# Attention with 10 of 17 blocks turned by TensorE, second key copies made by GpSimd, values in three 64-column products, and feed-forward weights at another remainder mod 512

## The chip, the cores and the metric

The kernel runs on one core of a Trainium2 chip. The metric is device microseconds of one execution, the median of the runs shown. Engine names are those of the profile: PE (TensorE matmul), PEld (TensorE weight load), DVE (VectorE), ACT (ScalarE), POOL (GpSimd), SP (SyncE, which issues most of the DMAs). Line numbers with an L are those of the kernel before.

## The reference, cut to what matters

One decoder layer for 2048 tokens of width 1024: a projection, eight attention heads of width 64 with a forget bias, a short gated convolution, an output projection, and a convolutional feed-forward of width 2816.

```python
logits = einsum('bqhd,bkhd->bhqk', qb, kb) * scale            # 128 queries, keys up to them
logits = logits + fcum[:, :, q0:q1, None] - fcum[:, :, None, :q1]
p = softmax(where(causal, logits, -inf))                      # over the key prefix
out = einsum('bhqk,bkhd->bqhd', p, vb)
...
u = causal_dwconv(h2 @ w_up, ffn_conv_w); y = (silu(u_gate) * u_val) @ w_down
```

Everything is float32. The kernel gets that precision by splitting an operand into a high and a low part (float32r for keys, queries and weights, float16 for the softmax weights and the values) and adding three products: high by high, high by low, low by high.

## The kernel before

**Stages.** The projections and the short convolution run to about 623 us of the span, attention from there to about 1025 us, the output projection (`mixed`, L853) with the second norm to about 1265 us, then twice the feed-forward's first product (`up`, L972, line L983 on PE) and second product (`down`, L1065, line L140 on PE).

**Attention's units.** A head is cut into 8 units. Unit `u` holds query block 15-u and query block u, which together have 17 blocks of 128 keys, so all 64 units have the same amount of work: five score chunks of up to 512 keys, 17 weight blocks of 128 x 128.

**Attention's steps.** The loop of L773 runs a software pipeline: in step `s` the generator `turn` works on unit s-2, `scores` on unit s, `weights` on unit s-1, `values` on unit s-4, a piece each in turn. `K` (L136) keeps the instructions of each engine in this program order; DMAs on SP are not pinned.
- `scores` (L672): `product` (L655) makes for each chunk two float32r products, L664 (key high parts) and L665 (key low parts), and a mask L667 for the last chunk. The contraction has 128 rows: rows 0 to 63 meet the query's high part, rows 64 to 127 its low part, so `kh` and `kl` hold the same 64 rows twice. Four PSUM banks (`ps_s`). DVE adds the forget bias `nf` and takes the running maximum (L688).
- `weights` (L698): ACT makes the exponential in place (L705).
- `turn` (L711): the 17 blocks of a unit must be transposed, in float16 high and low parts. The first `WB` = 6 go by PE (L726) into a PSUM bank of `ps_x` (two banks), ACT rounds the high part into `near` (L728), DVE makes the low part from the PSUM bank and the high part (L733), which frees the bank. The other 11 go another way: ACT (L709, the first 128 columns) and POOL (L718) round the high parts into `wide`, POOL subtracts for the low parts (L719), and one transposing DMA on SP (L720) carries both into `far`.
- `values` (L737): for each block a 128-column product of the high weights with the values' high and low parts side by side (L747) and a 64-column product of the low weights with the values' high part (L748). ACT scales the result into `at` (L752); its two 64-column halves are added later by DVE in `store` (L759), then transposed by PE (L764) and written out.

**Loads of the next head.** `load_head` (L557) gives seven DMAs on SP: `kh` twice, `qs` high and low, `kl` twice (64 x 2048 each, 512 KB) and `nf` (one row spread over 128 partitions, 1 MB). L787 issues one at each step u = 1 to 7 of the head before. The tiles have two buffers.

**Placement.** SBUF tiles on the right side lie below an `edge` tile of 32 bytes (L73). In the built program the feed-forward's weight tiles `hi` and `lo` (L825) start at remainder 448 mod 512 bytes, the operands `b11` to `t4` of `up` at remainder 0. In `down` and `mixed` both operands are halves of `hi` and `lo` tiles.

Of the kernel before, what the change touches and what calls it, by code (L numbers as in the profile page):

```python
# [19 lines left out]
P = 128  # L20
# [14 lines left out]
WB = 6  # L35
XA = 128
# [8 lines left out]
def kernel(  # L45
# [27 lines left out]
    edge.tile([P, 8], F32, name="edge")  # L73
# [73 lines left out]
    with ExitStack() as ph:  # L147
# [221 lines left out]
        p_ = bp.tile(n, F32, name="p_", bufs=1)  # L369
# [12 lines left out]
        V.scalar_tensor_tensor(p_, p_, -2.0, e_, op0=ALU.mult, op1=ALU.add)  # L382
        tri = bp.tile(n, F32, name="tri", bufs=1)
# [15 lines left out]
        def running_sum():  # L399
            pc = ps_t.tile([P, 512], F32, tag="tr", name="pc")  # L400
            K(T.matmul(pc[:, 0:P], lhsT=p_, rhs=tri, start=True, stop=True))
            V.tensor_copy(cum, pc[:, 0:P])
# [154 lines left out]
        def load_head(h):  # L557

            pr, r0 = h // 2, (h % 2) * DH
            r1 = r0 + DH  # L560
            tiles, loads = [], []
            for tag, srcs in (("kh", (k_hi, k_hi)), ("qs", (q_hi, q_lo)), ("kl", (k_lo, k_lo))):
                t = sp.tile([P, S], F32R, tag=tag, name=tag)
                for n, src in enumerate(srcs):
                    loads.append((t.bitcast(F32)[n * DH : (n + 1) * DH, :], src[r0:r1, pr, :]))
                tiles.append(t)
            t = sp.tile([P, S], F32, tag="nf", name="nf")
            loads.append((t, nf_sc[h].partition_broadcast(P)))
            return (*tiles, t), loads

        def issue(load):
            nc.sync.dma_start(*load)


        for j in range(4):
# [10 lines left out]
            for ch in range(4):  # L586
                if j == 3 and ch == 2:
                    hap.__exit__(None, None, None)
                    sp = st.enter_context(tc.tile_pool(name="sp", bufs=2, side="right"))
                    head, loads = load_head(0)  # L590
                    for ld in loads:
                        issue(ld)
# [34 lines left out]
    with ExitStack() as ph:  # L627
# [70 lines left out]
        def weights(un):  # L698

            s_t = un["s"]  # L700
            nb = cs.tile([P, 2], F32, tag="nb", name="nb")
            K(A.activation(nb, un["mx"], AF.Copy, scale=-1.0, bias=LN_PS))
            for p, (_, n, b0) in enumerate(un["parts"]):
                cols = s_t[:, b0 * P : (b0 + n) * P]
                K(A.activation(cols, cols, AF.Exp, bias=nb[:, p : p + 1], accum_out=un["l"][:, p : p + 1]))  # L705
                yield
            un["wide"] = wide = cp.tile([P, 2, WU - WB * P], F16, tag="wide", name="wide", bufs=3)
            if XA:
                K(A.activation(wide[:, 0, 0:XA], s_t[:, WB * P : WB * P + XA], AF.Copy))  # L709

        def turn(un):  # L711
# [6 lines left out]
            K(G.tensor_scalar(wide[:, 0, XA:], s_t[:, WB * P + XA : WU], 1.0, 0.0, op0=ALU.mult, op1=ALU.add))  # L718
# [3 lines left out]
            for b0 in range(0, WB, 4):  # L722
                nb = min(4, WB - b0)
                pt = ps_x.tile([P, 512], F32, tag="x", name="pt")
                for b in range(nb):
                    K(T.transpose(pt[:, b * P : (b + 1) * P], s_t[:, (b0 + b) * P : (b0 + b + 1) * P], ident))  # L726
                th, tl = [near[:, a, b0 : b0 + nb, :].rearrange("p b n -> p (b n)") for a in range(2)]
                K(A.activation(th, pt[:, 0 : nb * P], AF.Copy))  # L728
                late.append((tl, pt[:, 0 : nb * P], th))
            yield  # L730
            yield
            for tl, pt, th in late:
                K(V.tensor_tensor(tl, pt, th, op=ALU.subtract))  # L733
                yield
            K(V.reciprocal(un["l"], un["l"]))

        def values(un):  # L737
# [3 lines left out]
            for p, (i, n, b0) in enumerate(un["parts"]):  # L741
                po = ps_o.tile([P, P], F32, tag="o", name="po")
                for b in range(n):
# [3 lines left out]
                    K(T.matmul(po, lhsT=t[:, 0, :], rhs=v, start=b == 0, stop=False))  # L747
                    K(T.matmul(po[:, 0:DH], lhsT=t[:, 1, :], rhs=v[:, 0:DH], start=False, stop=b == n - 1))  # L748
                    if b % 4 == 3:
                        yield  # L750
                o = un["at"][:, i, :, (h % 2) * DH : (h % 2 + 1) * DH]
                K(A.activation(o, po.rearrange("p (a d) -> p a d", a=2), AF.Copy, scale=un["l"][:, p : p + 1]))  # L752
                yield

        def store(at, pr, chs):

            parts = [at[:, ch * 4 : ch * 4 + 4, :, :] for ch in chs]
            for part in parts:
                K(V.tensor_tensor(part[:, :, 0, :], part[:, :, 0, :], part[:, :, 1, :], op=ALU.add))  # L759
                yield  # L760
            for ch, part in zip(chs, parts):
                pt = ps_x.tile([P, 512], F32, tag="x", name="pt")
                for t in range(4):
                    K(T.transpose(pt[:, t * P : (t + 1) * P], part[:, t, 0, :], ident))  # L764
# [8 lines left out]
        for s in range(H * nu + 8):  # L773
            h, u = divmod(s, nu)
            run = []
            if h < H:
                if u == 0:
                    loads = []
                    if h + 1 < H:
                        heads[h + 1], loads = load_head(h + 1)  # L780
                    if h % 2 == 0:
                        if h:
                            v16.append(load_values(h // 2))
                        at = cp.tile([P, NT, 2, P], F32, tag="at", name="at")
# [342 lines left out]
```

## Time and profile before

| | |
|---|---|
| runs shown | 2614.63, 2619.37, 2624.09 us (median 2619.37) |
| the profiled execution, its own time | 2621.2 us |
| its span in the profile | 2619.5 us, so 1.7 us lie around it |
| PE busy | 2463.2 us, 94% of the span |
| DVE, ACT, POOL busy | 1800.2, 1142.5, 360.4 us |
| mean DMA rate | 161 GB/s |

Busy time of PE is a count of pipelined instructions, so 94% is not 94% of its peak; in a stretch without waits the start-to-start distance of matmuls is the price. The table is a mean over stages with different limits, so the stage that the change touches is read by itself, with the windows, waits, DMA and timeline views.

### The profile page before, as it was taken

What the parts mean: (1) busy time and instruction counts of PE and PEld (TensorE: products, weight loads), DVE (VectorE), ACT (ScalarE), POOL (GpSimd) and SP (SyncE); (2) the same over time, 40 slices, a digit from 0 to 9 for tenths busy, and PEclk for the clock granted to TensorE, in tenths of its full rate; (3) what the DMA queues carried; (4) which work ended last, traced back from release to release, by engine and by line L of the source; (5) the groups of instructions that cost most, each with busy time, mean ns of one, the idle gap of its engine ahead of it and who ended that gap; (6) DMA issues with size and microseconds to landing.
All of it is one profiled execution on the core that took longest, in us unless ns stands there. A gap on an engine that the chain in (4) does not pass through costs nothing.

```text
span 2619.5 us, 36119 instructions
## 1 busy us (share of the span) xinstructions
PE 2463.2 (94%) x13130; PEld 2017.2 (77%) x13130; DVE 1800.2 (69%) x3218; ACT 1142.5 (44%) x1880; POOL 360.4 (14%) x250
## 2 busy tenths in 40 slices
PE   4999999998887888886999999999999999999999
PEld 4987888886676667665788888877778888888887
DVE  7567864434776676458688888856858888886554
ACT  3522321113777675244344444445534444444333
POOL 4211111113666664000000000000000000000000
PEclk9999999999989899998999999999999999999999
DMA  8334663318999999886322222477652222226775
GB/s 246 123 122 120 191 197 116 109 61 210 207 211 217 221 211 227 277 304 226 112 88 74 89 81 81 136 243 232 193 184 73 89 81 81 89 75 189 225 229 191
DMA packets 490011, 420.99 MB, mean 161 GB/s; under 512 B 202000, under 2 KB 378472, under 8 KB 485736
## 3 DMA queue, kind: packets, MB, share of 16 engines
q1 hardware_dynamic: 482776, 406.03, 55.7%
q10 hardware_dynamic: 7056, 12.65, 1.4%
q8 instruction: 103, 1.69, 0.3%
q14 instruction: 76, 0.62, 0.1%
HBM read 294.80 MB, written 77.66 MB: 142 GB/s over the span
## 4 chain that ended last, share of the span: by engine, by line
PE 50%; DVE 3%; DMA 1%; ACT 1%; issue 0%; SPq 0%; DVEq 0%; ACTq 0%
PE acc L983 32%; PE acc L140 17%; DVE lo L841 1%; DMA raw<-m_at 0%; DMA t<-x_sc 0%; DVE t L850 0%; ACT junk L896 0%; PE pt L906 0%; DVE t L849 0%; ACT hi L840 0%; DMA x_sc<-t 0%; DVE t L928 0%; DVE t1l L841 0%; DVE t L927 0%; DVE t L923 0%
## 5 line engine op out<-in xcount | busy, mean ns | idle before, releaser
L841 DVE TENSOR_TENSOR lo<-raw,hi 128x1024 fp32r<-128x1024 f32 (+1 forms) x240 | 277.1, 1160 | 253.0 <-ACT hi L840 250.3
L840 ACT ACTIVATE hi<-raw 128x1024 fp32r<-128x1024 f32 (+1 forms) x240 | 239.3, 1002 | 377.6 <-PE acc L140 231.4
L140 PE MATMUL acc<-hi 128*128 128x512 f32 x960 | 376.2, 397 | 27.3 <-DVE t L849 10.4
L140 PE MATMUL acc<-lo,hi 128*128 128x512 f32 x960 | 380.6, 396 | 3.9 <-DVE lo L841 3.4
L140 PE MATMUL acc<-hi,lo 128*128 128x512 f32 x960 | 379.8, 396 | 1.9 <-DMA lo<-m_lo 1.8
L996 DVE SCALAR_TENSOR_TENSOR w<-w,fcw,w 128x1024 f32<-128x1024 f32 x176 | 225.9, 1283 | 37.6 <-ACT w L991 34.3
L140 PEld LDWEIGHTS acc<-hi 128*128 128x128 f32 x960 | 181.9, 190 | 72.7 <-ACT hi L840 16.5
L935 ACT ACTIVATE hi<-raw 128x1024 fp32r<-128x1024 f32 x132 | 139.6, 1059 | 214.3 <-PE acc L983 205.7
L140 PEld LDWEIGHTS acc<-lo,hi 128*128 128x128 f32 x960 | 183.1, 191 | 44.1 <-DVE lo L841 7.3
L140 PEld LDWEIGHTS acc<-hi,lo 128*128 128x128 f32 x960 | 182.9, 191 | 42.6 <-DMA lo<-m_lo 5.1
L719 POOL TENSOR_TENSOR wide<-s_t,wide 128x1408 f16<-128x1408 f32 x64 | 184.6, 2885 | 5.4
L938 DVE TENSOR_TENSOR lo<-raw,hi 128x1024 fp32r<-128x1024 f32 x132 | 160.9, 1220 | 13.2 <-ACT hi L935 13.2
L664 PE MATMUL ps<-kh,qs 128*128 128x512 f32 (+1 forms) x320 | 142.7, 446 | 18.3 <-DVE mx L688 17.5
L705 ACT ACTIVATE s_t<-s_t,nb 128x2048 f32<-128x2048 f32 (+15 forms) x128 | 152.9, 1196 | 5.7
L140 PE MATMUL pr<-hh,wh 128*128 128x512 f32 x384 | 153.3, 399 | 0.0
L140 PE MATMUL pr<-hl,wh 128*128 128x512 f32 x384 | 151.0, 393 | 0.0
L140 PE MATMUL pr<-hh,wl 128*128 128x512 f32 x384 | 150.9, 393 | 0.0
L688 DVE CUSTOM_DVE_ANT_0 s_t<-ps,nf,mx 128x512 f32<-128x512 f32 (+1 forms) x192 | 123.4, 643 | 29.0 <-PE ps L667 26.3
L665 PE MATMUL ps<-kl,qs 128*128 128x512 f32 (+1 forms) x320 | 122.5, 386 | 4.4 <-DMA kl<-k_lo 4.4
L688 DVE CUSTOM_DVE_ANT_0 s_t<-ps,nf 128x512 f32<-128x512 f32 (+3 forms) x128 | 78.4, 638 | 69.8 <-PE ps L665 31.5
L747 PE MATMUL po<-v,far 128*128 128x128 f16 x704 | 90.6, 233 | 34.4 <-DMA far<-wide 34.1
L747 PEld LDWEIGHTS <-far 128*128 128x128 f16 x704 | 68.0, 105 | 51.0 <-DMA far<-wide 37.5
(268 smaller groups left out, 5883.4 us busy)
## 6 DMA issues: line engine op xcount, KB each, us to landing
raw<-in_w_up_dram SPq DMA_DIRECT2D x88, 512.0 KB, 3.8
raw<-y_sc SPq DMA_DIRECT2D x176, 256.0 KB, 4.1
raw<-in_w_down_dram SPq DMA_DIRECT2D x176, 256.0 KB, 4.3
y_sc<-w SPq DMA_DIRECT2D x44, 512.0 KB, 2.6
wm<-in_w_ada_dram SPq DMA_DIRECT2D x128, 128.0 KB, 2.9
raw<-in_w_out_dram SPq DMA_DIRECT2D x64, 256.0 KB, 5.3
wr<-in_w_in_dram SPq DMA_DIRECT2D x40, 256.0 KB, 3.8
x_t<-in_x_dram SPq DMA_DIRECT2D x16, 512.0 KB, 5.3
```

The lines of the kernel that those rows point to most:

```text
L140: ins = T.matmul(acc, lhsT=a, rhs=b, start=st, stop=sp)
L664: K(T.matmul(ps[:, 0:cw], lhsT=qt, rhs=kh[:, c0 : c0 + cw], start=True, stop=False))
L688: K(V.tensor_tensor_reduce(out=s_t[:, o0 + c0 : o0 + c0 + cw], in0=ps[:, 0:cw], in1=nf[:, c0 : c0 + cw], scale=1.0, scalar=-3.0e38 if g == ...
L705: K(A.activation(cols, cols, AF.Exp, bias=nb[:, p : p + 1], accum_out=un["l"][:, p : p + 1]))
L719: K(G.tensor_tensor(wide[:, 1, :], s_t[:, WB * P : WU], wide[:, 0, :], op=ALU.subtract))
L747: K(T.matmul(po, lhsT=t[:, 0, :], rhs=v, start=b == 0, stop=False))
L840: A.activation(hi, raw, AF.Copy, scale=HS)
L841: V.tensor_tensor(lo, raw, hi.bitcast(F32), op=ALU.subtract)
L935: K(A.activation(hi, raw, AF.Copy, scale=HS))
L938: K(V.tensor_tensor(lo, raw, hi.bitcast(F32), op=ALU.subtract))
L983: K(T.matmul(acc, lhsT=a, rhs=b, start=st, stop=sp, skip_group_check=True))
L996: K(V.scalar_tensor_tensor(y, u[:, m : m + 1024], fcw[:, m * 44 + ct : m * 44 + ct + 1], y, op0=ALU.mult, op1=ALU.add))
```

## The change

Seven edits, most of them in attention:
1. `WB` goes from 6 to 10: PE transposes ten blocks per unit in groups of 4, 4 and 2, the transposing DMA carries 7 instead of 11. POOL does all the rounding of `wide`; ACT's L709 is gone (`XA`).
2. `turn` spreads its work over the step: two groups at the first piece, the third group at the third piece after the first subtraction has been written, subtractions one per piece.
3. `values` makes three 64-column products per block, all into the same 64 columns, so the two halves need no addition.
4. `at` is half as wide, `store` has no addition, ACT's result copy is 64 columns wide.
5. `kh` and `kl` are loaded once; POOL copies rows 0 to 63 to rows 64 to 127. The steps of the next head are five DMAs (u = 1 to 5) and two POOL copies (u = 6 and 7).
6. The `edge` tile has 480 bytes: `hi` and `lo` start at remainder 0 mod 512, as the operands of `up` do. Keys, queries and the first half of the projection's `h` tiles move with them.
7. In the forget gate's logarithm the result is written over `fg`, and `tri` shares the buffer of `p_`.

```diff
-WB = 6
-XA = 128
+WB = 10
-    edge.tile([P, 8], F32, name="edge")
+    edge.tile([P, 120], F32, name="edge")
...
-            for tag, srcs in (("kh", (k_hi, k_hi)), ("qs", (q_hi, q_lo)), ("kl", (k_lo, k_lo))):
+            for tag, srcs in (("kh", (k_hi,)), ("qs", (q_hi, q_lo)), ("kl", (k_lo,))):
...
+            for k in (tiles[0], tiles[2]):
+                steps.append(lambda k=k: K(G.tensor_scalar(k[DH:P, :], k.bitcast(F32)[0:DH, :], 1.0, 0.0, op0=ALU.mult, op1=ALU.add)))
...
-            if XA:
-                K(A.activation(wide[:, 0, 0:XA], s_t[:, WB * P : WB * P + XA], AF.Copy))
...
-            K(G.tensor_scalar(wide[:, 0, XA:], s_t[:, WB * P + XA : WU], 1.0, 0.0, op0=ALU.mult, op1=ALU.add))
+            K(G.tensor_scalar(wide[:, 0, :], s_t[:, WB * P : WU], 1.0, 0.0, op0=ALU.mult, op1=ALU.add))
...
+            def rest():
+                tl, pt, th = late.pop(0)
+                K(V.tensor_tensor(tl, pt, th, op=ALU.subtract))
+
+            blocks(0)
+            blocks(4)
             yield
+            rest()
             yield
-            for tl, pt, th in late:
-                K(V.tensor_tensor(tl, pt, th, op=ALU.subtract))
-                yield
+            blocks(8)
+            rest()
+            yield
+            rest()
+            yield
...
-                    K(T.matmul(po, lhsT=t[:, 0, :], rhs=v, start=b == 0, stop=False))
-                    K(T.matmul(po[:, 0:DH], lhsT=t[:, 1, :], rhs=v[:, 0:DH], start=False, stop=b == n - 1))
+                    vh, vl = v[:, 0:DH], v[:, DH:P]
+                    K(T.matmul(po, lhsT=t[:, 0, :], rhs=vh, start=b == 0, stop=False))
+                    K(T.matmul(po, lhsT=t[:, 0, :], rhs=vl, start=False, stop=False))
+                    K(T.matmul(po, lhsT=t[:, 1, :], rhs=vh, start=False, stop=b == n - 1))
...
-            for part in parts:
-                K(V.tensor_tensor(part[:, :, 0, :], part[:, :, 0, :], part[:, :, 1, :], op=ALU.add))
-                yield
...
-                    if u <= len(loads):
-                        issue(loads[u - 1])
+                    steps[u - 1]()
```

How the change moves instructions is read from the order of the two built programs, at three places; line numbers in the pieces of the changed kernel are its own.

On PE in the middle of a step of attention, before: the value products of one block (`po`, from `far`), then all six transposes (`pt`), then the values of the next part.

```order
L747 LDWEIGHTS far
L747 MATMUL po<-v_7316,far 128x128
L748 LDWEIGHTS far
L748 MATMUL po<-v_7316,far 128x64
L726 MATMUL pt<-ident,s_t 128x128 x6
L747 LDWEIGHTS near
L747 MATMUL po<-v_7316,near 128x128
```

The same engine after, at the third piece of a step: one block of values with three loads and three products, the two transposes of the third group, and the next score chunks behind them.

```order
L756 LDWEIGHTS near
L756 MATMUL po<-v_7603,near 128x64
L757 LDWEIGHTS near
L757 MATMUL po<-v_7603,near 128x64
L758 LDWEIGHTS near
L758 MATMUL po<-v_7603,near 128x64
L724 MATMUL pt<-ident,s_t 128x128 x2
L663 MATMUL ps<-kh,qs 128x512
L664 MATMUL ps<-kl,qs 128x512
```

Each block has one weight load more; the high weights are loaded twice in a row. The third group now stands ahead of score products on PE, and waits for a bank of `ps_x`.

On DVE one step of attention before: score chunks (L688, each with a read of its maximum), the two subtractions L733 of the low parts, the reciprocal. The step's fifth chunk follows.

```order
L688 ISA s_t,mx<-ps,nf 128x512
L688 ISA mx 128x1
L688 ISA s_t,mx<-ps,nf 128x384
L688 ISA mx 128x1
L733 TENSOR_TENSOR near<-pt,near 128x512
L688 ISA s_t,mx<-ps,nf,mx 128x512
L688 ISA mx 128x1
L733 TENSOR_TENSOR near<-pt,near 128x256
L688 ISA s_t,mx<-ps,nf,mx 128x512
L688 ISA mx 128x1
L735 RECIPROCAL l<-l 128x2
```

The same step after.

```order
L687 ISA s_t,mx<-ps,nf 128x512
L687 ISA mx 128x1
L731 TENSOR_TENSOR near<-pt,near 128x512
L687 ISA s_t,mx<-ps,nf 128x384
L687 ISA mx 128x1
L731 TENSOR_TENSOR near<-pt,near 128x512
L687 ISA s_t,mx<-ps,nf,mx 128x512
L687 ISA mx 128x1
L731 TENSOR_TENSOR near<-pt,near 128x256
L687 ISA s_t,mx<-ps,nf,mx 128x512
L687 ISA mx 128x1
L743 RECIPROCAL l<-l 128x2
```

There is one subtraction of 512 columns more, and the first comes one chunk earlier.

On POOL at the end of a head, after: the two key copies stand between the `wide` pieces of two steps. Before, only the pairs of `wide` stand there.

```order
L570 TENSOR_SCALAR kh<-kh 64x2048
L715 TENSOR_SCALAR wide<-s_t 128x896
L716 TENSOR_TENSOR wide<-s_t,wide 128x896
L570 TENSOR_SCALAR kl<-kl 64x2048
L715 TENSOR_SCALAR wide<-s_t 128x896
L716 TENSOR_TENSOR wide<-s_t,wide 128x896
```

The two copies are new on this engine, each ahead of a step's `wide` pieces, and the next head's first score products read both of their results.

More of the change, by code (lines that the diff above doesn't have):

```diff
@@ L368 @@
         s_ = bp.tile(n, F32, tag="s_", name="s_", bufs=1)
-        p_ = bp.tile(n, F32, name="p_", bufs=1)
+        p_ = bp.tile(n, F32, tag="p_", name="p_", bufs=1)
         V.tensor_scalar(e_, f2, -1.0, None, op0=ALU.mult)
@@ L381 @@
         V.tensor_scalar(e_, f2, 0.0, None, op0=ALU.min)
-        V.scalar_tensor_tensor(p_, p_, -2.0, e_, op0=ALU.mult, op1=ALU.add)
-        tri = bp.tile(n, F32, name="tri", bufs=1)
+        V.scalar_tensor_tensor(f2, p_, -2.0, e_, op0=ALU.mult, op1=ALU.add)
+        tri = bp.tile(n, F32, tag="p_", name="tri", bufs=1)
         G.affine_select(out=tri, in_=ones, pattern=[[1, P]], compare_op=ALU.is_ge, fill=0.0, base=0, channel_multiplier=-1)
@@ L400, in running_sum @@
             pc = ps_t.tile([P, 512], F32, tag="tr", name="pc")
-            K(T.matmul(pc[:, 0:P], lhsT=p_, rhs=tri, start=True, stop=True))
+            K(T.matmul(pc[:, 0:P], lhsT=f2, rhs=tri, start=True, stop=True))
             V.tensor_copy(cum, pc[:, 0:P])
@@ L560, in load_head @@
             r1 = r0 + DH
-            tiles, loads = [], []
-            for tag, srcs in (("kh", (k_hi, k_hi)), ("qs", (q_hi, q_lo)), ("kl", (k_lo, k_lo))):
+            tiles, steps = [], []
+            load = lambda *a: steps.append(lambda: nc.sync.dma_start(*a))
+            for tag, srcs in (("kh", (k_hi,)), ("qs", (q_hi, q_lo)), ("kl", (k_lo,))):
                 t = sp.tile([P, S], F32R, tag=tag, name=tag)
                 for n, src in enumerate(srcs):
-                    loads.append((t.bitcast(F32)[n * DH : (n + 1) * DH, :], src[r0:r1, pr, :]))
+                    load(t.bitcast(F32)[n * DH : (n + 1) * DH, :], src[r0:r1, pr, :])
                 tiles.append(t)
             t = sp.tile([P, S], F32, tag="nf", name="nf")
[L568 to L572, printed above, removed]
+            load(t, nf_sc[h].partition_broadcast(P))
+            for k in (tiles[0], tiles[2]):
+                steps.append(lambda k=k: K(G.tensor_scalar(k[DH:P, :], k.bitcast(F32)[0:DH, :], 1.0, 0.0, op0=ALU.mult, op1=ALU.add)))
+            return (*tiles, t), steps
         for j in range(4):
@@ L589 @@
                     sp = st.enter_context(tc.tile_pool(name="sp", bufs=2, side="right"))
-                    head, loads = load_head(0)
-                    for ld in loads:
-                        issue(ld)
+                    head, steps = load_head(0)
+                    for step in steps:
+                        step()
                 pr = {}
@@ L721, in turn, with blocks @@
             late = []
-            for b0 in range(0, WB, 4):
+            def blocks(b0):
                 nb = min(4, WB - b0)
@@ L777 @@
                 if u == 0:
-                    loads = []
+                    steps = []
                     if h + 1 < H:
-                        heads[h + 1], loads = load_head(h + 1)
+                        heads[h + 1], steps = load_head(h + 1)
                     if h % 2 == 0:
```

13 lines of the change are left out of this document (6 added, 7 removed).

## The prediction

> **What bounds the kernel now.** First the page: the span, and in its 40 slices the lines of PE, of the granted clock and of the DMA engines.
>
> ```profile
> span 2619.5 us, 36119 instructions
> ...
> PE   4999999998887888886999999999999999999999
> ...
> PEclk9999999999989899998999999999999999999999
> DMA  8334663318999999886322222477652222226775
> ```
>
> A slice is 65 us. In slices 10 to 16, attention, the DMA engines are at 9 and PE falls to 8; almost everywhere else PE is at 9. So attention is looked at by itself, with the windows view. From the start of the first score chunk on DVE (625.5) to that of the last unit (998.7) there are 63 steps; the second row is the last head's seven steps, the third one undisturbed step, the fourth one step at the change from head 4 to 5.
>
> ```profile
> core 0: us, PE busy (x) PEld busy (x) DVE busy (x) ACT busy (x) POOL busy (x), PEclk, DMA share, GB/s
> 625.50:998.70 373.20, 315.87 (x3165) 252.30 (x3165) 263.13 (x827) 268.45 (x623) 252.40 (x123) 0.92 1.09 210
> 966.10:998.70 32.60, 31.78 (x331) 26.07 (x331) 27.94 (x92) 25.39 (x61) 23.38 (x12) 0.91 0.91 158
> 929.30:933.50 4.20, 4.20 (x53) 3.56 (x51) 4.08 (x16) 3.77 (x9) 3.11 (x2) 1.00 0.94 193
> 855.70:866.00 10.30, 8.20 (x91) 6.23 (x89) 4.18 (x14) 8.63 (x20) 4.71 (x3) 0.98 1.04 258
> ```
>
> A step takes 373.2/63 = 5.92 us on average, 32.6/7 = 4.66 in the last head, and 4.2 where nothing disturbs, with PE and DVE both full. The last head differs in one thing: no loads of a next head run. So 63 x (5.92 - 4.66) = 79 us of attention are disturbance. The waits of the same window say by whom.
>
> ```profile
> PEld L747 <- DMA far<-wide: 33.9, 19, 4.2
> DVE s_t L688 <- PE ps L665: 31.5, 27, 8.0
> PE po L747 <- DMA far<-wide: 30.9, 17, 4.0
> DVE s_t L688 <- DMA nf<-nf_sc: 27.5, 4, 7.7
> ```
>
> PE waits some 31 us for transposed weights, and DVE 27.5 us at four changes of head for `nf`, the last of the seven loads, with PE stopped behind it. Both are transfers that come late on full DMA engines: the DMA view of the window, then that of the last head alone.
>
> ```profile
> q1 hardware_dynamic: 178688, 77.34, 108.3%
> ...
> nf<-nf_sc SPq DMA_DIRECT2D x7, 1024.0 KB
> kl<-k_lo SPq DMA_DIRECT2D x13, 512.0 KB, 5.4
> kh<-k_hi SPq DMA_DIRECT2D x12, 512.0 KB, 5.8
> ...
> far<-wide SPq DMA_TRANSPOSE x61, 7.1
> ```
> ```profile
> q1 hardware_dynamic: 19260, 5.10, 90.8%
> ...
> far<-wide SPq DMA_TRANSPOSE x8, 7.0
> ```
>
> In the last head eight transposes take 0.908 x 32.6 = 29.6 us of the sixteen engines, 3.7 us each. In the whole window 61 x 3.7 = 226 us are transposes out of 1.083 x 373.2 = 404; the other 178 are loads and stores.
>
> **The change, part by part.** *Transfers (edits 1 and 5).* A transpose shrinks from 11 blocks to 7: 61 x 3.7 x 7/11 = 144 us. Half of the 25 loads of `kl` and `kh` go, 6 MB of some 32 MB that are not transposes (estimate, from counts and sizes of the issues), so 178 becomes some 145. Together 289 us where 404 were; at the 108% that the window sustained that is 267 us, under the 321 that the steps will need (below). The DMAs stop being the limit, `far` comes earlier, and `nf` is issued at u = 5 instead of 7, two steps ahead of its use. The 79 us of disturbance go, but not to zero: I leave 8 us (estimate: a little over 1 us at each of seven head changes), with 0 and 35 (under half of them remain) as ends.
>
> *PE.* Four transposes more per unit, and a load more per block.
>
> ```profile
> 869.92 0.22 PE L747 MATMUL po<-v,far 128*128 128x128 f16 x1
> 869.97 0.19 PE L748 MATMUL po<-v,far 128*128 128x64 f16 x1
> 870.00 0.22 PE L747 MATMUL po<-v,far 128*128 128x128 f16 x1
> ...
> 870.26 0.22 PE L747 MATMUL po<-v,far 128*128 128x128 f16 x1
> 870.31 0.19 PE L748 MATMUL po<-v,far 128*128 128x64 f16 x1
> ```
> ```profile
> 870.34 0.85 PE L726 MATMUL pt<-ident,s_t 128*128 128x128 f32 x6
> ```
>
> From 869.92 to 870.26 four blocks pass, 0.085 us each; the 64-column product holds the array for only 0.03 us (869.97 to 870.00), and the load for the product behind it lies within that. Three such products are 0.085 to 0.09 us: the same as now, so I take nothing for the values. No row shows two of them in a row, so the bound on the other side is a load that cannot follow so closely: two loads fit in 0.085 us, at most 0.0425 each, three 0.128. The Trainium skill (page "TensorE: Matmul & The Clock Gate", LDWEIGHTS and weight-path modes) has a rule that speaks against this edit: a weight load takes its columns at 1.2 GHz, 107 ns for 128, and about half with its fast load as measured there. By that rule three loads would be 160 ns or more per block, the step 6.4 us and the time 2653; the trace already has two loads in 85 ns, so that figure does not hold here. The transposes: six take 0.85 us with the last one's 0.27 of drain, 0.116 us apart, so four more are 0.46 us per step.
>
> *DVE, ACT, POOL.*
>
> ```profile
> L728 ACT ACTIVATE near<-pt 128x512 f16<-128x512 f32 x61 | 36.4, 596 | 6.9 <-PE pt L726 3.6
> ...
> L709 ACT ACTIVATE wide<-s_t 128x128 f16<-128x128 f32 x62 | 18.3, 296 | 8.0 <-DMA far<-wide 7.8
> ```
> ```profile
> L733 DVE TENSOR_TENSOR near<-pt,near x128: 409/550/694, 633.1 to 1009.8; 128x512 f16<-128x512 f32 x64, 128x256 f16<-128x256 f32 x64
> ```
> ```profile
> L759 DVE TENSOR_TENSOR at<-at x16: 682/941/3009, 715.6 to 1024.1; 128x512 f32<-128x512 f32 x16
> ```
> ```profile
> L719 POOL TENSOR_TENSOR wide<-s_t,wide 128x1408 f16<-128x1408 f32 x64 | 184.6, 2885 | 5.4
> L718 POOL TENSOR_SCALAR wide<-s_t 128x1280 f16<-128x1280 f32 x64 | 81.0, 1265 | 122.3 <-ACT s_t L705 84.9 <-DMA far<-wide 12.2 <-DVE at L759 11.3
> ...
> L134 POOL TENSOR_SCALAR th<-tf 128x512 fp32r<-128x512 f32 x32 | 20.1, 627 | 170.6 <-ACT tf L469 170.5
> ```
>
> DVE gains one subtraction of up to 0.69 us per step and loses the additions, 16 x 0.94 = 15 us in all. From 27.94/7 = 3.99 us a step it goes to about 4.68. ACT gains 0.60, loses 0.30, and its result copies halve: from 25.39/7 = 3.63 to about 3.9. POOL falls from 4.15 to 2.7 us (both pieces in proportion to their columns); a key copy of 2048 columns at L134's rate is 2.5 us, twice per head, 0.6 a step. POOL stays the idlest. In the last step of a head the `kl` copy stands ahead of that step's `wide` pieces and sends its transpose off 2.5 us later; `far` has two steps, so that hides. Were it not hidden, the cost is at most 2 x 2.5 us per head, 35 us.
>
> *The step.* Now 4.66 us undisturbed. PE is the engine that fills it (31.78 of 32.60), so its extra 0.46 is added: 5.12 us. Lower end: DVE alone, 4.68. Upper end: DVE's extra 0.69 in full on top, 5.35.
>
> *Placement (edit 6).* The chain of waits holds `up` and `down` as two long pieces of PE; a chunk of the convolution, 72 matmuls, lies between two rows of DVE.
>
> ```profile
> 1265.52 424.39 PE acc L983 x1846
> 1689.92 51.83 PE acc L140 x228
> ```
> ```profile
> 600.61 0.69 DVE L607 TENSOR_TENSOR z<-z,pr 128x512 f32<-128x512 f32 x1 [8.44 <-PE pr L140]
> ```
> ```profile
> 617.28 0.69 DVE L607 TENSOR_TENSOR z<-z,pr 128x512 f32<-128x512 f32 x1 [8.44 <-PE pr L140]
> ```
>
> A matmul of the same shape takes 424.39/1846 = 229.9 ns in `up`, 51.83/228 = 227.3 in `down`, and 16.67/72 = 231.5 in the convolution, where the weights' remainders mod 512 go through all of eight values. In `down` both operands have the same remainder, as `up` will have. So `up` may gain 2.6 ns x 3696 products = 9.6 us, or lose 1.6 x 3696 = 6 where the convolution is the model. I take -6, nearer to `down`, since part of the 2.6 can be waits inside the long piece. `down` and `mixed` keep equal remainders: nothing. Weight tiles of the projection have all remainders before and after: nothing.
>
> *The rest.* Head 0's two copies wait on POOL for DMAs issued at 589 us; POOL is idle there.
>
> ```profile
> 601.47 1.56 POOL L615 TENSOR_SCALAR y<-z,cst 128x512 f32<-128x512 f32 x1 [14.94 <-DVE z L607]
> ```
>
> It has 14.9 us between two convolution pieces, so 2 x 2.5 us cost nothing; without that cover, 5 us. `tri` behind the logarithm costs nothing either: POOL's next work is L134, which waits 170 us in all for ACT.
>
> The sum: 63 x 5.12 = 322.6, plus 8 of remaining disturbance, is 331 where 373.2 stood: -42. With -6 of placement, -48. The profiled execution's own time is 2621.2, 1.8 above the median of the runs: **2573 us**.
>
> **The rivals.** *Disturbance stays.* If late transfers are a matter of queueing behind 512 KB loads and not of the total, 35 us of the 79 remain, and the step is at its upper end: 63 x 5.35 + 35 = 372, almost no gain in attention; the first alone gives 2600, the second alone 2587. For it: five loads still share SP's queue with the transposes. Against: the shares above. In between, 2600: 0.14.
>
> *The load bounds the values.* At 0.128 us per block the step grows by 17 x 0.043 = 0.73 to 5.85 us, 63 x 5.85 + 8 = 377: with placement, 2619, no change. The trace bears it out no further than that bound. 0.07.
>
> *Slower: PE waits for its bank.* The third group needs the bank of the first, which frees after ACT's copy (0.60) and DVE's subtraction (0.69). PE has score chunks and eight blocks of values between, enough if ACT takes the copy at once. ACT runs in order, with the exponentials in front; if the copy comes only as PE arrives, PE stands 1.3 us each step, with its score chunks queued behind: 63 x 6.42 + 8 = 412, 2654. It decides from about a microsecond of lag of ACT. Against: ACT is free a fifth of a step. 0.08.
>
> *Placement is worth nothing or costs*, attention as forecast: 2579 to 2585: 0.05, inside the forecast's side.
>
> **How the numbers follow.** The forecast, 2545 to 2595, has 0.66. The range takes in the disturbance case and reaches down to nearly the lower step (63 x 4.68 = 295, no remainder, -9.6: 2533): 2543 to 2606. Above it lie most of the load case and the bank case. Faster by over 0.3% (8 us, about what a measurement of this kernel can tell from no change): 0.66 + 0.14 + 0.05 and a little of the load case, 0.87; within 0.3%: 0.05; slower: 0.08.
>
> **What would show it.** Right: the last head's steps near 5.1 us, the others hardly longer; no wait of DVE for `nf`; waits for `far` under 10 us; DMA share in attention near 0.9; value blocks 0.085 us apart; `up` near 227.5 ns per matmul. Wrong: products of one block 0.04 us apart; PE waiting for L731 ahead of the third group; a product waiting for POOL's `kl`; DMA share still at 1.1.

## The result and the profile after

| | before | after |
|---|---|---|
| median of the runs | 2620.25 us | 2562.49 us (2559.79 to 2563.71) |
| the profiled execution, its own time | 2621.2 us | 2563.71 us |
| its span | 2619.5 us | 2562.0 us |

The ratio after to before is 0.978, with an interval of 0.976 to 0.980. In the rows below the line numbers of the changed kernel are its own: L724 the transposes on PE, L726 ACT's copy of a group, L731 DVE's subtraction, L687 DVE's reading of a score chunk, L704 the exponentials, L715 and L716 POOL's rounding, L756 to L758 the value products, L762 ACT's copy of a result, L988 `up`.

First the page, with the same lines as before:

```profile
span 2562.0 us, 38669 instructions
...
PE   4999999999999998897999999999999999999999
...
PEclk9999999999999999998999999999999999999999
DMA  8433674316799958886222222676642222226776
```

The stretch of slices in which PE stood at 8 with the DMA engines at 9 is gone. The windows view gives attention by the same landmarks as before, from the first score chunk on DVE to that of the last unit (63 steps), and the last head's seven steps:

```profile
core 0: us, PE busy (x) PEld busy (x) DVE busy (x) ACT busy (x) POOL busy (x), PEclk, DMA share, GB/s
626.70:955.40 328.70, 322.88 (x4423) 263.25 (x4423) 286.13 (x874) 281.01 (x623) 200.99 (x138) 1.00 0.85 168
919.10:955.40 36.30, 35.73 (x508) 29.15 (x507) 32.15 (x99) 30.67 (x69) 19.81 (x15) 1.00 0.52 90
```

A step takes 328.7/63 = 5.22 us where it took 5.92, and 36.3/7 = 5.19 in the last head. So the loads of the next head no longer disturb: from the second head on the steps at one position in the head differ by some 0.5 us at most (4.6 to 6.2 us each, by the position), and none of the 8 to 14 us of before is left. The granted clock in this window is 1.00, where it was 0.92; the DMA share is 0.85. The DMA view of the window, then of the last head:

```profile
q1 hardware_dynamic: 117689, 54.02, 83.9%
...
far<-wide SPq DMA_TRANSPOSE x61, 4.4
```
```profile
q1 hardware_dynamic: 12651, 3.19, 51.8%
...
far<-wide SPq DMA_TRANSPOSE x7, 4.0
```

Of the waits in that window these are the ones that bear on the prediction:

```profile
DVE near L731 <- ACT near L726: 39.0, 60, 1.1
...
PEld pt L724 <- DVE near L731: 12.0, 42, 0.9
...
PE pt L724 <- DVE near L731: 2.2, 6, 0.5
```

No wait for `far` or for `nf` is left. New is a chain of small waits around the transposes' banks: DVE waits 39.0 us for ACT's copies, and PE's weight load 12.0 us for DVE's subtractions (PE's own row, 2.2, belongs to the same waits, so the two are not added).

Where the 57.5 us of the two profiled executions lie: the scores (first to last score product) take 333.5 us instead of 378.5, -45.0; the values behind the last score 17.8 instead of 20.8, -3.0; the output projection and second norm, from the last value product to the first product of `up`, 231.7 instead of 238.3, -6.6; the two `up` -5.2; attention starts 1.4 later, and the rest is +0.9. The 6.6 us are not put down to the change: over the kernels below, none of which touches that stage in its code, it takes from 227.8 to 237.2 us in their single profiles.

### The profile page after: what moved, and what is told of

Same layout as the page of the kernel before. It is cut to its first block, busy times and chain, and to the rows that moved or that the text cites. A ratio compares the mean times of both kernels' runs of the same rounds, so it can differ in the third digit from the quotient of the medians.

```text
span 2562.0 us, 38669 instructions
## 1 busy us (share of the span) xinstructions
PE 2461.8 (96%) x14474; PEld 2030.1 (79%) x14474; DVE 1819.8 (71%) x3266; ACT 1154.9 (45%) x1880; POOL 309.6 (12%) x266
## 4 chain that ended last, share of the span: by engine, by line
PE 51%; DVE 3%; DMA 1%; ACT 1%; issue 1%; SPq 0%; ACTq 0%; DVEq 0%
PE acc L988 33%; PE acc L139 17%; DVE lo L846 1%; DMA raw<-m_at 0%; PE pt L911 0%; DMA t<-x_sc 0%; DVE t L854 0%; DVE t L855 0%; ACT hi L845 0%; DMA t<-in_x_dram 0%; DMA hi<-m_hi 0%; ACT junk L901 0%; ACT t L913 0%; DVE t4l L846 0%; DVE b22l L846 0%
## 5 line engine op out<-in xcount | busy, mean ns | idle before, releaser
L704 ACT ACTIVATE s_t<-s_t,nb 128x2048 f32<-128x2048 f32 (+15 forms) x128 | 152.9, 1196 | 5.7
L731 DVE TENSOR_TENSOR near<-pt,near 128x512 f16<-128x512 f32 (+1 forms) x192 | 115.0, 600 | 43.7 <-ACT near L726 42.8
L663 PE MATMUL ps<-kh,qs 128*128 128x512 f32 (+1 forms) x320 | 133.8, 419 | 1.9 <-DVE mx L687 1.1
L687 DVE CUSTOM_DVE_ANT_0 s_t<-ps,nf,mx 128x512 f32<-128x512 f32 (+1 forms) x192 | 123.2, 642 | 2.6
L716 POOL TENSOR_TENSOR wide<-s_t,wide 128x896 f16<-128x896 f32 x64 | 121.5, 1899 | 5.4
L664 PE MATMUL ps<-kl,qs 128*128 128x512 f32 (+1 forms) x320 | 115.5, 365 | 0.0
L724 PE MATMUL pt<-ident,s_t 128*128 128x128 f32 x640 | 101.2, 283 | 6.8 <-DVE near L731 4.4
L139 PE MATMUL acc<-wh,hh 128*128 128x512 f32 x256 | 103.3, 404 | 0.0
```

The lines of the kernel that those rows point to most:

```text
L139: ins = T.matmul(acc, lhsT=a, rhs=b, start=st, stop=sp)
L663: K(T.matmul(ps[:, 0:cw], lhsT=qt, rhs=kh[:, c0 : c0 + cw], start=True, stop=False))
L664: K(T.matmul(ps[:, 0:cw], lhsT=qt, rhs=kl[:, c0 : c0 + cw], start=False, stop=not last))
L687: K(V.tensor_tensor_reduce(out=s_t[:, o0 + c0 : o0 + c0 + cw], in0=ps[:, 0:cw], in1=nf[:, c0 : c0 + cw], scale=1.0, scalar=-3.0e38 if g == ...
L716: K(G.tensor_tensor(wide[:, 1, :], s_t[:, WB * P : WU], wide[:, 0, :], op=ALU.subtract))
```

## The experiments

**Do transfers limit?** Three kernels. The first undoes the halved key loads alone:

```diff
-("kh", (k_hi,)), ("qs", (q_hi, q_lo)), ("kl", (k_lo,))
+("kh", (k_hi, k_hi)), ("qs", (q_hi, q_lo)), ("kl", (k_lo, k_lo))
...
-            for k in (tiles[0], tiles[2]):
-                steps.append(lambda k=k: K(G.tensor_scalar(k[DH:P, :], ...)))
```

> The changed kernel with edit 5 undone: kh and kl are loaded twice each, seven loads per head, nf again the last at u = 7, no key copies on POOL. Prediction's theory (the sum of transfers decides): the stage's DMA work is 0.85 x 328.7 = 279 us of sixteen engines in the changed kernel, and the twelve extra loads add some 33 (estimate of the prediction), 312 in 329 us, share 0.95 and below the 1.08 that the kernel before sustained; so the step stays near 5.22 us, waits for far under 10 us, and the time is 2560 to 2570. Rival (late transfers are a matter of queueing behind 512 KB loads and of nf being last): DVE waits for nf again, 20 to 27 us at the changes of head, and the time is 2580 to 2595.

Measured: 2563.69 us, ratio 0.9777 [0.9742, 0.9812], the same as the changed kernel. The window of the 63 steps, 627.2 to 955.9 (the last but one number is the DMA share):

```profile
627.20:955.90 328.70, 322.92 (x4423) 263.37 (x4424) 286.07 (x876) 281.30 (x623) 174.78 (x124) 1.00 0.98 194
```

The share is 0.98 instead of 0.85, with the same 328.7 us. The twelve loads cost some 43 us of the sixteen engines, not 33. No wait for `nf` or `far` came back, with `nf` again the last load. So the loads and their place in the queue do not delay by themselves: a share of 0.98 costs nothing here. With ten turned blocks the key copies on POOL buy nothing.

The second undoes edits 1 and 2 (six transposes on PE again, in two groups) and keeps the rest:

```diff
-WB = 10
+WB = 6
...
             un["wide"] = wide = cp.tile(...)
+            K(A.activation(wide[:, 0, 0:P], s_t[:, WB * P : WB * P + P], AF.Copy))
...
-            blocks(4)
-            yield
-            rest()
-            yield
-            blocks(8)
-            rest()
+            blocks(4)
+            yield
+            yield
+            rest()
```

> The changed kernel with edits 1 and 2 undone: PE transposes 6 of 17 blocks, the transposing DMA carries 11, ACT's L709 is back; edit 5 (half the key loads, nf at u = 5) stays. Sum-of-transfers theory: 61 x 3.7 = 226 us of transposes plus the 116 us that the changed kernel has beside them is 342 us; at a share of 1.02 to 1.08 that takes 317 to 335 us, where PE alone would need 63 x 4.66 = 294: transfers limit again, step 5.0 to 5.3, share over 1.0, far waits of 20 us or more, time 2550 to 2570, so more transposes on PE bought little over edit 5 alone. Queueing theory (edit 5 alone removes the disturbance): step 4.7 to 4.8, time 2530 to 2540. Ring theory (PE, ACT and DVE wait for each other over the two banks of ps_x) expects only that DVE's wait for ACT's L726 nearly goes, since there is no third group.

Measured: 2590.56 us, ratio 0.988 [0.985, 0.991], step 5.52 us. Window and waits of the 63 steps:

```profile
628.50:976.60 348.10, 301.92 (x4166) 245.26 (x4165) 253.65 (x815) 262.40 (x623) 278.65 (x137) 0.96 1.05 202
```
```profile
PEld L755 <- DMA far<-wide: 46.3, 24, 6.4
...
PE po L755 <- DMA far<-wide: 43.5, 24, 6.3
DVE s_t L687 <- PE ps L664: 36.9, 32, 6.9
```

Transfers limit, as the sum says: share 1.05, PE some 45 us in waits for `far` (PE and its weight load stand in the same wait, so the two rows are not added), DVE behind it; single steps take up to 13 us beside others of 4.2. It is worse than the 317 to 335 us that the sum gave, because the transfers are more than the 342 us it took: 1.05 x 348.1 = 366, which at a share of 1.02 to 1.08 needs 339 to 359. (A transpose of eleven blocks was priced too low, see below.) That the size of the transposes alone does it is ruled out by the last head of the same kernel, which has transposes of eleven blocks and no loads:

```profile
944.47:976.59 32.12, 32.12 (x487) 26.65 (x483) 27.94 (x91) 28.92 (x71) 28.99 (x15) 1.00 0.89 165
```

PE is busy all the time there, with no wait for `far`, and a step takes 4.59 us. DVE's wait for ACT's copies is 13.0 us, a third of the changed kernel's, near what the ring theory expected without a third group. Against the kernel before with only the placement changed (step 5.85, below) the step is 0.32 us shorter: with six blocks, edits 3 to 5 together are worth 63 x 0.32 = 20 us; the same edits are worth nothing with ten.

The third turns eight blocks, in two groups, so that no group needs a bank that its own unit still holds:

```diff
-WB = 10
+WB = 8
...
             blocks(0)
             blocks(4)
             yield
             rest()
             yield
-            blocks(8)
-            rest()
-            yield
             rest()
             yield
```

> Eight of 17 blocks by TensorE in two groups of four, so no third group: two transposes, one copy of 256 columns and one subtraction of 256 columns less, and nine blocks by the transposing DMA instead of seven. If VectorE's chain sets the step, it is 4.57 - 0.34 = 4.23 us of work without the wait, TensorE at about 4.9 takes over: step 4.7 to 4.95 us and 2532 to 2548 us, provided the DMA engines keep up (nine blocks are 3.0 us of them per step, loads 2.3). The rival: transfers are the limit again, waits for far and nf return, and the time is 2565 us or more.

Measured: 2557.59 us, ratio 0.975 [0.9709, 0.9792]; step 5.07 us. Its DMA rows in the window of the 63 steps:

```profile
q1 hardware_dynamic: 146679, 61.40, 101.2%
...
far<-wide SPq DMA_TRANSPOSE x61, 6.4
```

It lies between the two expectations, 2532 to 2548 and 2565 or more. At a share of 1.02 waits for `far` are back (16.4 us on PE's weight load), and the step is 5.07 on average; in the last head, without loads, it is 4.72, as the first expectation had it. So the two limits cross near eight or nine blocks.

**Do the narrow value products cost?** The kernel with edits 3 and 4 undone:

```diff
-                    K(T.matmul(po, lhsT=t[:, 0, :], rhs=vh, start=b == 0, stop=False))
-                    K(T.matmul(po, lhsT=t[:, 0, :], rhs=vl, start=False, stop=False))
-                    K(T.matmul(po, lhsT=t[:, 1, :], rhs=vh, start=False, stop=b == n - 1))
+                    K(T.matmul(po, lhsT=t[:, 0, :], rhs=v, start=b == 0, stop=False))
+                    K(T.matmul(po[:, 0:DH], lhsT=t[:, 1, :], rhs=v[:, 0:DH], start=False, stop=b == n - 1))
...
+            for part in parts:
+                K(V.tensor_tensor(part[:, :, 0, :], part[:, :, 0, :], part[:, :, 1, :], op=ALU.add))
+                yield
...
```

> The changed kernel with edits 3 and 4 undone: a 128-column and a 64-column product per block, at twice as wide, DVE's additions in store and ACT's wide result copy are back. If PE alone sets the step (5.12 us in the prediction): value blocks 0.085 us apart as before, nothing lost, 2560 to 2567. If DVE's work counts in the step (ring theory): the additions, 16 x 0.94 = 15 us, and ACT's copies, which grow by 0.05 to 0.1 us each, push the stage out by 10 to 18 us, 2573 to 2582. If three narrow products are in truth dearer than the two: the time falls, 2555 or less.

Measured: three runs of 2561.4 to 2561.9 us (a fourth took 4953 us and is left out), ratio 0.9771 [0.9737, 0.9806]: no difference. The step is 5.21 us. DVE's busy time in the window rose to 294.0 us, 8 more, and its wait for ACT's copies fell to 30.9, 8 less:

```profile
626.50:955.00 328.50, 320.34 (x3420) 260.15 (x3421) 294.04 (x888) 286.63 (x623) 202.01 (x138) 1.00 0.83 168
```
```profile
DVE near L731 <- ACT near L726: 30.9, 55, 1.1
```

The additions went into waiting time. So DVE's waits are no proof that DVE's work sets the step: the expectation of the ring theory, 10 to 18 us more, was wrong here. That value blocks cost the same either way is seen in the timeline of the changed kernel, where the starts of one line are 0.09 us apart:

```profile
834.68 0.19 PE L757 MATMUL po<-v,near 128*128 128x64 f16 x1
834.71 0.19 PE L758 MATMUL po<-v,near 128*128 128x64 f16 x1
834.74 0.19 PE L756 MATMUL po<-v,near 128*128 128x64 f16 x1
834.77 0.19 PE L757 MATMUL po<-v,near 128*128 128x64 f16 x1
```

**What sets the step of 5.22 us?** One place of the changed kernel in the timeline shows the chain:

```profile
925.33 2.01 ACT L704 ACTIVATE s_t<-s_t,nb 128x2048 f32<-128x2048 f32 x1
...
926.02 0.42 PE L724 MATMUL pt<-ident,s_t 128*128 128x128 f32 x2
...
927.34 0.39 ACT L704 ACTIVATE s_t<-s_t,nb 128x128 f32<-128x128 f32 x1
...
927.72 0.36 ACT L726 ACTIVATE near<-pt 128x256 f16<-128x256 f32 x1
...
928.09 1.16 PE L724 MATMUL pt<-ident,s_t 128*128 128x128 f32 x8
928.11 0.42 DVE L731 TENSOR_TENSOR near<-pt,near 128x256 f16<-128x256 f32 x1 [0.76 <-ACT near L726]
928.45 0.74 DVE L687 CUSTOM_DVE_ANT_0 s_t<-ps,nf,mx 128x512 f32<-128x512 f32 x1
```

PE has the third group ready at 926.4, but ACT is in the exponentials until 927.7; DVE stands 0.76 us for the copy, with the next score chunk queued behind; and the second of the next unit's groups on PE needs the bank that this subtraction frees. Two theories: PE's own work makes 5.2 us, and these waits cost nothing; or the three engines wait for each other in a ring over the two banks, and the waits lengthen the step. Three kernels move a part of it, two more give it another bank. The third group's transposes a piece earlier, so that its copy comes between the exponentials:

```diff
             rest()
-            yield
             blocks(8)
+            yield
             rest()
```

> The third group of transposes one piece earlier, so that on ScalarE its copy stands between the two exponentials instead of behind both. If VectorE's chain sets the step (4.57 us of work and 0.65 us of waiting for that copy), the wait falls to 0.1 to 0.3 us, the step to 4.7 to 4.9 us, and the time to 2540 to 2550 us. If TensorE's own work sets it at 5.12 us, as the prediction had it, the wait falls but the step stays at 5.1 or more: 2556 us or above.

Measured: 2573.06 us, ratio 0.9811 [0.9775, 0.9847], step 5.38 us. The copy did come earlier, but DVE's wait did not fall, as both expectations had it, and PE's rose; the waits of the 63 steps:

```profile
DVE near L731 <- ACT near L726: 43.1, 79, 0.9
...
PEld pt L724 <- DVE near L731: 24.5, 32, 1.9
...
PE pt L724 <- DVE near L731: 20.1, 31, 1.6
```

Now PE stands before the third group until the first subtraction has freed the bank, and the step grew with PE's wait. The groups in the order 2, 4, 4 instead of 4, 4, 2:

```diff
-                nb = min(4, WB - b0)
+                nb = min(4, WB - b0) if b0 else 2
...
-            blocks(4)
+            blocks(2)
...
-            blocks(8)
+            blocks(6)
```

> The changed kernel with the groups of turned blocks in the order 2, 4, 4 in place of 4, 4, 2: the third group takes the bank of a group of two, whose copy on ACT (0.36 against 0.60 us) and subtraction on DVE (0.42 against 0.69) are shorter, so that bank comes free some 0.5 us earlier. Ring theory, with PE's wait for the bank as the link that binds: PE's waits for L731 (12.0 us on PEld, 2.2 on PE) go, step 5.0 to 5.1, 2550 to 2558. Ring theory, with ACT's third copy as the link that binds: that copy is now 0.60 instead of 0.36 and DVE waits longer for it, 39 us become 50 or more, step 5.3 to 5.45, 2568 to 2580. PE's own work sets the step: 5.2 as before, 2560 to 2567.

Measured: 2570.92 us, ratio 0.9807 [0.9778, 0.9836], step 5.34 us, DVE's wait for L726 49.0 us, that of PE's weight load for L731 20.3. The second form of the ring came true: the longer third copy counts, not the earlier bank, and PE's wait for the bank rose instead of going. The third subtraction a piece later, behind the fourth score chunk:

```diff
             blocks(8)
             rest()
             yield
+            yield
             rest()
```

> The changed kernel with the third subtraction a piece later, so that DVE reads the fourth score chunk while ACT still has the exponentials ahead of the third copy. Ring theory with DVE's wait for that copy as the link that binds: DVE's 39 us of waits for L726 fall below 15, step 4.9 to 5.1, 2543 to 2556. Ring theory in its other form (as in the two kernels that moved the third group, the wait is only passed on: the bank of the third group comes free later, PE stands longer): PE's 14 us of waits for L731 become 25 or more, step 5.2 to 5.4, 2560 to 2575. PE's own work sets the step: 5.2, 2560 to 2567.

Measured: 2558.90 us (2550.73 to 2559.34), ratio 0.975 [0.9726, 0.9774], step 5.10 us. Its window and waits:

```profile
626.10:947.60 321.50, 317.81 (x4420) 261.13 (x4420) 286.30 (x875) 279.68 (x622) 200.57 (x137) 1.00 0.87 171
```
```profile
DVE near L731 <- ACT near L726: 29.0, 71, 0.8
...
PEld pt L724 <- DVE near L731: 6.8, 22, 1.0
```

One instruction of DVE moved past another, no work changed, and the stage is 7.2 us shorter. That is far beyond its noise: in the profiles of the changed kernel and of the three kernels here that change neither the groups nor their order (the loads twice, the wide values, the old placement) the stage takes 328.5 to 328.7 us. The times of the whole kernel do not show it as well: the median is 3.6 us lower, the intervals of the two ratios overlap, and the profiled execution, 2550.73, is 8 us faster than the other three. So the step of the changed kernel is not PE's work alone. DVE's wait fell by 10 us, less than expected, and that of PE's weight load for the bank nearly by half; the step came out at the upper edge of what was expected, and the time above its 2543 to 2556. Over these three kernels and the changed one the step goes with the waits of PE's weight load for L731: 6.8, 12.0, 20.3 and 24.5 us stand beside 5.10, 5.22, 5.34 and 5.38. Between the first and the last the waits grow by 17.7 us and the stage by 338.9 - 321.5 = 17.4.

A third bank for the transposes, taken from the value products, alone and with the later subtraction:

```diff
-        ps_x = ph.enter_context(tc.tile_pool(name="ps_x", bufs=2, space=PSUM))
-        ps_o = ph.enter_context(tc.tile_pool(name="ps_o", bufs=2, space=PSUM))
+        ps_x = ph.enter_context(tc.tile_pool(name="ps_x", bufs=3, space=PSUM))
+        ps_o = ph.enter_context(tc.tile_pool(name="ps_o", bufs=1, space=PSUM))
```

> The changed kernel with three banks for the transposes (ps_x) and one, in place of two, for the value products (ps_o). Ring theory with the bank as the link that binds: PE's 14 us of waits for L731 go, step 4.95 to 5.05 less what the single ps_o bank costs (PE may wait for ACT's L762, up to 0.3 us twice a step). Ring theory with DVE's wait for ACT as the link: DVE's busy 4.54 plus 0.62 of wait stay, step 5.15 to 5.25, 2558 to 2567. If the single ps_o bank costs more than the third one brings, the step is 5.3 or more with waits of PE for L762 in the list.

> Both at once: three banks for the transposes, one for the value products, and the third subtraction a piece later. If the ring over the banks sets the step, both of its waits are now gone: step near PE's own work, which is 4.72 (the last head with eight turned blocks) + 2 x 0.116 = 4.95 us, or up to 5.05 with the single ps_o bank: 2541 to 2552. If PE's own work were 5.2, nothing: 2560 to 2567.

Measured: 2586.06 us, ratio 0.9865 [0.9841, 0.9889], step 5.52 us, and 2580.05, ratio 0.9842 [0.9818, 0.9866], step 5.49. The waits of the first:

```profile
DVE near L731 <- ACT near L726: 57.6, 72, 1.2
...
PEld L757 <- issue: 28.9, 39, 1.1
PE po L756 <- ACT at L762: 25.5, 39, 1.0
```

As the third expectation had it, PE's wait for L731 is gone from the list, and a longer one for ACT's copy of the result stands in its place. The single result bank costs more than the third transpose bank brought, so neither theory is settled by these two, and whether three banks with two result banks would do more is open.

**Placement.** The changed kernel with the old `edge` tile, and the kernel before with the new one (with edit 7, which makes room for it):

```diff
-    edge.tile([P, 120], F32, name="edge")
+    edge.tile([P, 8], F32, name="edge")
```

> The changed kernel with the edge tile at 32 bytes again, so that the feed-forward's weights stand at remainder 448 as before. If placement is worth what the two traces show in the long pieces (228.9 against 226.7 ns between matmuls of the first feed-forward product, some 5 us after more waiting), the time is 2567 to 2569 us, and the output projection stays 6 to 7 us shorter than before. The rival, that placement made all of the 14 us gained behind attention, gives 2576 us and an output projection as long as before. If placement is worth nothing: 2562 us.

> The kernel before with the edge tile at 480 bytes and the forget gate's buffers shared (which makes room for it), and nothing else. Placement worth 5 us: ratio 0.998, matmuls of the first feed-forward product 226.7 ns apart. The rival with placement worth 14 us: ratio 0.9945. Worth nothing: 1.000. If sharing the forget gate's buffers is what makes attention start 1.3 us later, it starts 1.3 us later here too.

Measured: without the new placement 2571.94 us, ratio 0.9815 [0.9778, 0.9853], 9.4 above the changed kernel (the ranges of the runs, 2571.07 to 2581.77 and 2559.79 to 2563.71, lie apart, the intervals of the ratios overlap); the placement alone 2611.33, ratio 0.9955 [0.9937, 0.9972], 7.8 below the 2619.15 of its comparison. Both lie between the 5 us and the 14 us of the expectations. With the placement alone the two `up`, from first to last product, are together 8.2 us shorter than before, and attention starts 0.4 us later, not 1.3: the shared buffers do not explain the later start of the changed kernel. Attention's step is 5.22 us in the first, as in the changed kernel, and 5.85 in the second, where before had 5.92. The two pieces of `up` in the chains of waits, first of the changed kernel, then with the old placement, then of the placement alone:

```profile
1212.91 421.55 PE acc L988 x1846
...
1895.96 421.38 PE acc L988 x1846
```
```profile
1217.30 425.58 PE acc L988 x1846
...
1903.10 432.29 PE acc L988 x1846
```
```profile
1257.89 420.33 PE acc L983 x1846
...
1939.31 420.32 PE acc L983 x1846
```

Before it was 424.39 both times. With equal remainders a piece takes 420 to 422 us; with unequal ones 424 to 426, or 432. The profiled execution with the old placement, 2581.77, is 10 us slower than the other three, and the long second piece is most of that.

**Both findings together.** The later subtraction, and nine turned blocks, groups of 4, 4 and 1:

```diff
-WB = 10
+WB = 9
...
             blocks(8)
             rest()
             yield
+            yield
             rest()
```

> The kernel with the third subtraction a piece later, and with nine turned blocks (groups of 4, 4 and 1; the transposing DMA carries eight). Work per step against that kernel: one transpose less on PE (0.116 us), ACT's copy and DVE's subtraction of 128 columns instead of 256 (by the rows of 512 and 256 columns, 0.60 and 0.36, 0.69 and 0.42, some 0.12 and 0.13 less: an estimate). Ring theory (work of PE and DVE plus their waits for each other make the step): step 5.10 - 0.12 = 4.95 to 5.02, 2547 to 2555. Transfers theory: 0.87 x 321.5 = 280 us become some 304 (between this and the 326 of the kernel with eight blocks), share 0.96 in 316 us, so waits for far stay under 15 us; if they are 25 us or more and the step stays at 5.1, transfers limit earlier than their share says, 2557 to 2563.

Measured: 2550.98 us (2545.01 to 2554.26), ratio 0.974 [0.9721, 0.9759], the fastest here, 11.5 below the changed kernel. The step is 5.00 us:

```profile
626.20:941.00 314.80, 308.99 (x4357) 254.27 (x4357) 279.01 (x875) 273.02 (x622) 222.01 (x137) 1.00 0.98 187
```
```profile
DVE near L731 <- ACT near L726: 28.4, 62, 0.9
...
PEld pt L724 <- DVE near L731: 4.0, 13, 0.9
...
PEld L757 <- DMA far<-wide: 2.5, 2, 1.6
```

The expectation held: 0.11 us less per step, a share of 0.98, almost no wait for `far`. The stage is shorter than that of ten blocks with the later subtraction (321.5) and of eight (319.7); the intervals of the three ratios overlap. All three limits are now close together, transfers at 0.98, PE busy 309 of 315 us, DVE's work and waits 307.

## Why the prediction was right, point by point

**Transfers: right in the limit, and lucky in the sum.** Attention was bound by transfers that came late, and that limit went. The sum of 289 us on the DMA engines measured 0.85 x 328.7 = 279, but both of its parts were off. A transpose of eleven blocks costs 4.3 us, not 3.7: the prediction divided the last head's 29.6 us by eight issues, while its 19260 packets, 256 bytes each but for a few, make only 6.8 transposes (22 blocks of 128 rows, 2816 packets each). In the changed kernel's last head seven transposes of 1792 packets take 0.518 x 36.3 = 18.8 us, 2.7 each. Per packet that is 24.6 and 23.8 ns of an engine, so a transpose does go in proportion to its blocks, as the prediction took it. Over the window the 256-byte packets took 255 us before and 181 after, all others 152 and 99. So the transposes were forecast 37 us too low (144) and the rest 46 too high (145), and the two errors nearly cancel.

**What the late transfers cost: more than the waits.** The prediction put the 79 us down to disturbance and did not look at the clock that its rows show, 0.92 on average before. A wait of PE and a stretch behind it, with the transposes in that stretch:

```profile
646.40:650.30 3.90, 0.03 (x2) 0.00 (x0) 1.40 (x6) 2.02 (x4) 2.15 (x1) 1.00 0.93 142
651.30:654.70 3.40, 3.40 (x21) 2.88 (x21) 1.32 (x4) 1.11 (x3) 3.26 (x2) 0.50 0.79 210
```
```profile
653.15 1.52 PE L726 MATMUL pt<-ident,s_t 128*128 128x128 f32 x6
```

The granted clock is half, and the six transposes take 1.52 us, where the prediction's row has 0.85. Over the 63 steps of before there are eleven such stretches, 61 us together, each beginning in a wait of PE of 1.5 us or more, or within 1 us behind it. So up to 31 of the 79 us were work at half clock and not waiting (an estimate: half of the 61). In the same 63 steps of the changed kernel there is none.

**Remaining disturbance: 8 us forecast, none measured.** That the last head's steps, 5.19, are as long as the others is the evidence.

**The step: 5.12 forecast, 5.22 measured. The price of the transposes held; a wait came on top.** The prediction added four transposes to a PE that it took to be full. The last heads, where no loads run, show what that is worth: a step takes 4.59 us with six turned blocks (all other edits in place), 4.72 with eight, 5.06 with ten and the later subtraction, and 5.19 in the changed kernel. From six to ten it is 0.47 us with the later subtraction, where 0.46 was forecast, though not evenly: 0.13 for the first two blocks, 0.34 for the other two, which come as a third group. The rest is waiting: with the later subtraction the same PE instructions take 5.10 over all steps, so at least 0.12 of the 5.22 is not PE's work; the waits for the bank are 12.0/63 = 0.19 us a step. This is the bank rival in a mild form. It had the right chain, ACT's copy behind the exponentials and DVE's subtraction behind the copy, and a price of 1.3 us where some 0.1 to 0.2 came. Its counter-evidence was that ACT is free a fifth of a step; ACT's 281.01/63 = 4.46 us, not the 3.9 forecast, leave a seventh. The 3.9 started from the last head's 3.63, while the whole window of before gave 268.45/63 = 4.26. The two errors, 63 x 0.10 = 6 us too little for the step and 8 too much for disturbance, nearly cancel, which is luck: 328.7 us where 331 was forecast.

**Values: right.** Three products of 64 columns are 0.088 us per block against 0.085, and undoing them changes nothing. The rule for weight loads that the prediction cited (the Trainium skill, page "TensorE: Matmul & The Clock Gate", LDWEIGHTS and weight-path modes) would have made it 160 ns or more, and here it does not hold as a price of the chain: a single load of 128 columns does last 0.10 us in the trace, but the loads overlap, and in the timeline above a product, each with a load of its own, starts every 30 ns or so.

**Placement: right in sign, small in size.** -6 was taken; 7.8 and 9.4 were measured, near the bound of 9.6, and 8.2 in the two `up` themselves with the placement alone. In the changed kernel's profile they are only 5.2 shorter, at the same distance of its products: some 3 us more are waits.

**Key copies on POOL: hidden, as said.** The group of POOL's row:

```profile
L570 POOL TENSOR_SCALAR kl<-kl 64x2048 fp32r<-64x2048 f32 x8 | 15.6, 1950 | 0.7
```

They take 1.9 us, not 2.5, and no engine waited for them. But the loads that they save were no cost with ten turned blocks: the kernel without the copies is as fast.

**Beside the sum.** -48 was forecast and -57.5 came. The 9.5 us in between, in these two executions: 3.0 from the scores (-45.0 for -42), 3.0 from the values behind the last score, 6.6 from the output projection, and back 0.8 from the two `up` (-5.2 for -6) and 2.3 from the rest. The projection's part stays without a cause. (The 2573 counts from the profiled execution, 2621.2 - 48; from the median of the runs it is 2571.)

## What to carry to other kernels

Where a shared limit is relieved in two ways, measure each with the other in place: half the key loads, with edits 3 and 4, was worth 20 us with six turned blocks and nothing with ten. Count what a late transfer costs with the clock that is granted behind the wait. When the limit goes, look at once at what the new work waits for: here a copy queued behind exponentials, and moving one subtraction behind a score chunk gave back a part of what the added transposes cost. The shortest stage of those tried had nine blocks and the later subtraction, where transfers, PE and the waits are about equal.

## What the runs showed of the hardware that was not expected

Outside of waits the start-to-start distance of `up`'s products is 226.7 ns in every kernel here that has weights and operands both at remainder 0 mod 512. That it is the equality and not the 0 that counts is borne out by `down`: there both stand at 448 in the kernel before and at 0 with the placement alone, and its products are 226 or 227 ns apart in both. Other remainders were not tried. With weights at 448 and operands at 0 it is 228.9 or 233.3 ns, and holds one of these for a whole half of the feed-forward: both halves 228.9 before, 228.9 and then 233.3 in the kernel with the old placement, 425.58 and 432.29 us for the same 1846 products. What chooses between them was not tried. A half at 233.3 is 1848 x 4.4 ns = 8 us longer, which may be part of the scatter of the kernel before.
